# A one-core decoder layer: output-projection factors of w_out built in two passes, the mixture stored by token halves, pointwise input split between the projections

## The chip, the cores and the metric

The kernel runs on one core of a Trainium2 chip. Its time is the device time of one execution in microseconds; the median of the runs is compared. The profile is one execution of the program, recorded by the hardware profiler. Engines are named as there: PE is TensorE (matrix products), DVE is VectorE, ACT is ScalarE, POOL is GpSimd, and SP is SyncE, which here issues all the loads and stores.

## The reference

One layer over 1024 tokens with 1024 channels, all in float32. What is computed:

```
u   = rms_norm(x, ln_g)
z   = u @ w_in                                   # 1024 x 7168, split in seven blocks of 1024
c_val, c_glu, c_gate, hq, hf, hi, hg = split(z)
y_conv = silu(group_layer_norm(causal_conv31(c_val * sigmoid(c_glu)) + conv_b))
y_conv = (y_conv @ w_pw2 + b_pw2) * silu(c_gate) # the pointwise projection
y_hgrn = rms_norm(gated_recurrence(hq, hf, hi)) * silu(hg)   # 8 heads of 128
h   = x + concat(y_conv, y_hgrn) @ w_out         # w_out is 2048 x 1024
pe  = p @ w_pp
h   = h + sigmoid(rms_norm(h, pe_norm_g) @ w_pg) * pe
out = rms_norm(h, final_g)
```

## The kernel before, in words

Every float32 product is made of three: each operand is split into a high part, rounded on ACT, and the rest, subtracted on DVE (`split`, lines 117 to 119), and PE adds high by high, high by low and low by high. On chip, channels stand in partitions and tokens in the free dimension, in tiles of 128 by 512.

The program has these stages. Up to about 738 us: the input norm, then for each of eight heads the blocks of z (`ztile`, 48 matmuls each: 8 channel blocks, 3 products, 2 token halves), the convolution and the recurrence. Their tiles are in the pool wk. The last blocks of z are the eight gates c_gate (`conv_gate`, lines 492 to 496, numbers 16 to 23), stored to DRAM as sg_d. Then follow, in the program's text, `combos` (line 553), the projection of the heads' mixture yh_d (lines 662 to 671), the pointwise projection (683 to 705), the projection of the other mixture mc_d (753 and 754), and the last gate with the final norm.

The projection with w_out is done by a Winograd form of Strassen's scheme: for two blocks of 128 tokens `project` makes seven products of 12 matmuls in place of eight. Its factors from the mixture (w11, s1, s2, s4, s3, w12, w22) are sums of blocks, made by `tokens` (line 606); its factors from w_out (a, t1, t2, d, t3, c, t4) are made by `combos` for the lower and the upper thousand rows of w_out in turn: of each four 128x512 blocks a, b, c, d of a k, t1 = a - b, t2 = -(t1 + d), t3 = d - b, t4 = t1 + d - c. Each factor is split into high and low: 56 tiles of 128x512 in the pool cb, 112 KB of each partition. They are placed on the right end of SBUF, above the memory of the heads that have ended. Rows of w_out are loaded 128x1024 at a time: those of the first `combos` into the ring "raw" of the pool wp, three buffers that also take the gates' weights from `prep` (line 121); those of the second into the ring "raw" of rg, two buffers.

`project` reads the mixture from DRAM as two tiles (channels 0 to 511 and 512 to 1023 of 256 tokens) through the ring "raw" of rg; its products are added to two tiles of x, hx, one buffer each, and stored as h_d. rg lies on the left, in the memory of wp and of u, which the last gate reads. After the four projections, the 16 tiles of y_conv (ycr) are loaded through the ring "s" of rg and split into ych and ycl, 32 tiles of yp that the pointwise projection reads. It runs over m, the block of 128 output channels; its result, times the gate, is stored as 128 rows of mc_d (line 705), and then all of h_d is loaded back.

The order on each engine is the tile framework's: it takes the program's order, changed by priorities (`high_priority`; AHEAD and SOON are such distances), and inserts the waits. A tile waits for the last use of what lay in its memory before, tile by tile. Each engine and SP run their instructions in that order, so a waiting load holds those behind it.

Of the kernel before, what the change touches and what calls it, by code (L numbers as in the profile page):

```python
# [16 lines left out]
P = 128  # L17
T = 1024
D = 1024
G = 8  # L20
# [10 lines left out]
AHEAD, SOON = 500, 1000  # L31
# [6 lines left out]
def trunk_kernel(ctx: ExitStack, tc: tile.TileContext, x, p, ln_g, w_in, conv_w, conv_b,  # L38
# [16 lines left out]
    def halves(t):  # L55
        return t[:, :H], t[:, H:]
# [8 lines left out]
    mc_d = dpl.tile([D, T], F32, name="mc_d")  # L65
# [485 lines left out]
    cb = ctx.enter_context(tc.tile_pool(name="cb", bufs=1, side="right", reuse_waits="tile"))  # L551

    def combos(row0, pool, bufs):

        hi = {n: [] for n in XN}
        lo = {n: [] for n in XN}

        def part(n, k, src, sign=1.0):
            hi[n].append(cb.tile([P, H], F32R, tag=f"{n}h{k}", name=f"{n}h{row0}_{k}"))
            lo[n].append(cb.tile([P, H], F32R, tag=f"{n}l{k}", name=f"{n}l{row0}_{k}"))  # L560
            h = hi[n][k]
            nc.scalar.activation(h, src, AF.Copy, scale=sign)
            nc.vector.scalar_tensor_tensor(lo[n][k], src, sign, h.bitcast(F32),
                                           op0=ALU.mult, op1=ALU.subtract)

        for k in range(KH):
            rows = []
            for i in range(2):
                r = pool.tile([P, D], F32, tag="raw", bufs=bufs, name=f"wo{row0}_{k}_{i}")
                o = row0 + (i * KH + k) * P  # L570
                nc.sync.dma_start(r, w_out[o:o + P, :])
                rows += halves(r)
            a, b, c, d = rows
            for n, t in (("a", a), ("c", c), ("d", d)):
                part(n, k, t)
            nc.vector.tensor_tensor(a, a, b, op=ALU.subtract)
            part("t1", k, a)
            nc.vector.tensor_tensor(a, a, d, op=ALU.add)
            part("t2", k, a, -1.0)
            nc.vector.tensor_tensor(b, d, b, op=ALU.subtract)  # L580
            part("t3", k, b)
            nc.vector.tensor_tensor(c, a, c, op=ALU.subtract)
            part("t4", k, c)
        return hi, lo

    for m in range(G // 2):
        conv_gate(m)
    xh, xl = combos(D, wp, 3)
# [4 lines left out]
    rg = ctx.enter_context(tc.tile_pool(name="rg", bufs=4, reuse_waits="tile"))  # L593
# [12 lines left out]
    def tokens(src, tb):  # L606

        r0, r1 = (raw(src[i * H:(i + 1) * H, tb * P:(tb + 2) * P]
                      .rearrange("(k p) t -> p k t", p=P), f"mx{src.name}{tb}_{i}")
                  for i in range(2))  # L610
        w11, w21, w12, w22 = r0[:, :, :P], r0[:, :, P:], r1[:, :, :P], r1[:, :, P:]

        def add(n, x, y):
            o = rg.tile([P, KH, P], F32, tag="s", name=f"s{src.name}{tb}_{n}")
# [7 lines left out]
        return [factor(f"f{src.name}{tb}_{n}", t)  # L622
                for n, t in enumerate((w11, s1, s2, s4, s3, w12, w22))]

    def project(src, tb, hA, hB):

        f1, f5, f6, f3, f7, f2, f4 = tokens(src, tb)
        za, zd, zb = (bank("z", f"o{n}{src.name}{tb}") for n in "adb")

# [32 lines left out]
    with tc.tile_pool(name="hx", bufs=1, reuse_waits="tile") as hx:  # L662
        for tb in range(0, G, 2):
# [8 lines left out]
        ych = [[None] * G, [None] * G]  # L672
        ycl = [[None] * G, [None] * G]
        for hf in range(2):
            for k in range(G):
                ych[hf][k] = yp.tile([P, H], F32R, tag="y", name=f"ych{hf}_{k}")
                ycl[hf][k] = yp.tile([P, H], F32R, tag="y", name=f"ycl{hf}_{k}")
                t = rg.tile([P, H], F32, tag="s", name=f"ycr{hf}_{k}")
                nc.sync.dma_start(t, yc_d[k][:, hf * H:(hf + 1) * H])
                split(ych[hf][k], ycl[hf][k], t)  # L680


    with tc.tile_pool(name="sp", bufs=2, reuse_waits="tile") as sgp:
        for m in range(G):
            if m == 1:
                xh, xl = combos(0, rg, 2)
# [18 lines left out]
            nc.sync.dma_start(mc_d[m * P:(m + 1) * P, :], sg)  # L705
# [9 lines left out]
    def norm_T(hf, tags):  # L715
# [3 lines left out]
        for k in range(G):  # L719
# [5 lines left out]
            hh[k] = cb.tile([P, H], F32R, tag=f"{n}h{kk}", name=f"hh{hf}_{k}")  # L725
            hl[k] = cb.tile([P, H], F32R, tag=f"{n}l{kk}", name=f"hl{hf}_{k}")
# [29 lines left out]
    hhA, hlA = norm_T(0, ("a", "t1"))  # L756
    gate_weights(1, lambda q, k, name: cb.tile([P, H], F32R, tag=f"{('t2', 'd')[k // KH]}{q}{k % KH}",
                                               name=name))
    hhB, hlB = norm_T(1, ("c", "t4"))
# [67 lines left out]
```

## Time and profile before

| what | us |
|---|---|
| median of 3 runs (lowest, highest) | 1214.06 (1213.29, 1214.9) |
| the profiled execution's own time | 1217.44 |
| its span, first to last instruction | 1215.6 |
| PE busy, share of the span | 1124.5, 92% |
| DVE busy | 817.2, 67% |
| ACT busy | 461.5, 38% |
| mean granted clock of PE | 0.965 |

Busy times are sums over an engine's instructions. The granted clock is a share of 2.4 GHz; the two levels that the rows show are the full one and half of it. In the page's slices a digit is the busy share of one fortieth of the span, 30.4 us, in tenths. In lists of waits a row gives the waiting engine, what it made, what it waited for, then the sum in us, how many times, and the longest.

### The profile page before, as it was taken

The numbers are of one execution on the slowest core, as the hardware profiler recorded it, in microseconds if no ns is written. First come the engines' busy times: TensorE is split into PE (matmuls) and PEld (weight loads), VectorE is DVE, ScalarE is ACT, GpSimd is POOL, SyncE is SP. The second block draws the span as 40 slices with busy tenths as digits, with TensorE's granted clock in tenths as the row PEclk, the third lists the DMA queues.
The fourth block names the chain that finished last, engine by engine and source line by source line (L and its number), as shares of the span: only waits on it lengthen the run. The fifth ranks groups of instructions, "written<-read, shape, count | busy, mean of one in ns | idle before, by whom it ended". The sixth has DMA issues, their size and how long they took to land.

```text
span 1215.6 us, 17917 instructions
## 1 busy us (share of the span) xinstructions
PE 1124.5 (92%) x7312; PEld 935.9 (77%) x7312; DVE 817.2 (67%) x1305; ACT 461.5 (38%) x867; POOL 73.2 (6%) x107
## 2 busy tenths in 40 slices
PE   7999999999999999999999992688996994999997
PEld 5889888789788898888988882576675883887886
DVE  4669399995799965999849946405476721566644
ACT  4732254532443433435335325302143310226533
POOL 3100001010010100100100100000000000000100
PEclk9999999999999999999999996798997997999999
DMA  7511111211211121121121213324367545223221
GB/s 253 203 52 35 53 53 54 69 53 36 70 52 54 36 63 59 36 69 37 53 61 45 88 53 104 104 80 130 137 233 233 191 138 207 70 88 121 70 104 70
DMA packets 94547, 112.98 MB, mean 93 GB/s; under 512 B 3930, under 2 KB 74586, under 8 KB 94466
## 3 DMA queue, kind: packets, MB, share of 16 engines
q1 hardware_dynamic: 94466, 111.85, 28.2%
q8 instruction: 57, 0.93, 0.3%
q14 instruction: 24, 0.20, 0.0%
HBM read 82.48 MB, written 29.36 MB: 92 GB/s over the span
## 4 chain that ended last, share of the span: by engine, by line
PE 77%; DVE 10%; DMA 10%; ACT 2%; issue 1%; SPq 1%; POOL 0%; POOLq 0%; DVEq 0%; ACTq 0%
PE z L246 13%; PE z L247 13%; PE z L248 13%; DVE y L457 4%; PE v L270 3%; PE v L269 3%; PE v L268 3%; PE pw L700 3%; PE pw L701 2%; PE pw L702 2%; PE pg L780 2%; PE pg L779 2%; PE pg L778 2%; DMA mxyh_d<-yh_d 1%; PE sc L300 1%; DMA mxmc_d<-mc_d 1%
## 5 line engine op out<-in xcount | busy, mean ns | idle before, releaser
L457 DVE SCALAR_TENSOR_TENSOR y<-vpad,par,y 128x1024 f32<-128x1024 f32 x232 | 288.7, 1278 | 1.1
L778 PE MATMUL pg<-gh,hh 128*128 128x512 f32 (+1 forms) x136 | 52.3, 385 | 1.6 <-ACT hh L727 1.6
L779 PE MATMUL pg<-gl,hh 128*128 128x512 f32 (+1 forms) x136 | 52.4, 385 | 0.0
L780 PE MATMUL pg<-gh,hl 128*128 128x512 f32 (+1 forms) x136 | 52.1, 383 | 0.0
L524 DVE TENSOR_TENSOR vpad<-z,gl 128x512 f32<-128x512 f32 x16 | 11.0, 690 | 42.7 <-PE z L248 42.7
L246 PE MATMUL z<-uh,wz20h 128*128 128x512 f32 x16 | 7.6, 474 | 32.1 <-ACT wz20h L118 32.1
L700 PE MATMUL pw<-ych,wpw_0h 128*128 128x512 f32 x64 | 26.0, 407 | 11.6 <-ACT wpw_0h L118 11.6
L268 PE MATMUL v<-wv_0h,uh 128*128 128x256 f32 x128 | 36.7, 287 | 0.0
L270 PE MATMUL v<-wv_0h,ul 128*128 128x256 f32 x128 | 36.5, 285 | 0.0
L269 PE MATMUL v<-wv_0l,uh 128*128 128x256 f32 x128 | 36.5, 285 | 0.0
L270 PE MATMUL v<-wv_1h,ul 128*128 128x256 f32 x128 | 36.2, 283 | 0.0
L268 PE MATMUL v<-wv_1h,uh 128*128 128x256 f32 x128 | 36.2, 283 | 0.0
L269 PE MATMUL v<-wv_1l,uh 128*128 128x256 f32 x128 | 36.2, 283 | 0.0
L271 ACT ACTIVATE vt<-v 128x256 f32<-128x256 f32 x32 | 12.2, 382 | 59.0 <-PE v L270 59.0
L784 DVE TENSOR_TENSOR gt<-gt,pet 128x512 f32<-128x512 f32 (+1 forms) x17 | 11.2, 661 | 33.9 <-ACT gt L783 33.9
L480 DVE TENSOR_SCALAR y<-yt,mv,ry 128x128 f32<-128x128 f32 x64 | 23.5, 403 | 13.1 <-POOL ry L114 13.1
L113 POOL TENSOR_SCALAR ro<-sso 128x8 f32<-128x8 f32 x8 | 8.4, 1055 | 389.0 <-ACT on L134 389.0
L704 DVE SCALAR_TENSOR_TENSOR sgr<-pw,par,sgr 128x512 f32<-128x512 f32 x16 | 12.0, 747 | 29.3 <-PE pw L702 29.3
L778 PEld LDWEIGHTS pg<-gh,hh 128*128 128x128 f32 x136 | 25.8, 189 | 6.9 <-ACT hh L727 1.8
L442 ACT ACTIVATE on<-o,ro 128x128 f32<-128x128 f32 x64 | 18.6, 387 | 29.6 <-POOL ro L114 29.6
L779 PEld LDWEIGHTS pg<-gl,hh 128*128 128x128 f32 x136 | 25.8, 189 | 4.9
L780 PEld LDWEIGHTS pg<-gh,hl 128*128 128x128 f32 x136 | 25.7, 189 | 5.0
(698 smaller groups left out, 3551.5 us busy)
## 6 DMA issues: line engine op xcount, KB each, us to landing
wz<-in_w_in_dram SPq DMA_DIRECT2D x48, 512.0 KB
wo<-in_w_out_dram SPq DMA_DIRECT2D x16, 512.0 KB
xt<-in_x_dram SPq DMA_DIRECT2D x8, 512.0 KB
pe_d<-pes SPq DMA_DIRECT2D x8, 512.0 KB
wv<-in_w_in_dram SPq DMA_DIRECT2D x8, 512.0 KB
yc_d<-yc SPq DMA_DIRECT2D x8, 512.0 KB
yh_d<-sgT SPq DMA_DIRECT2D x8, 512.0 KB
sg_d<-sgc SPq DMA_DIRECT2D x8, 512.0 KB
```

Of the source, the lines that this page charges most:

```text
L246: mm(z, lhsT=wh[:, k, :], rhs=mh[hf][k], start=k == 0, stop=False)
L247: mm(z, lhsT=wh[:, k, :], rhs=ml[hf][k], start=False, stop=False)
L248: mm(z, lhsT=wl[:, k, :], rhs=mh[hf][k], start=False, stop=k == G - 1)
L268: mm(z, lhsT=uh[hf][k][:, c], rhs=wh, start=k == 0, stop=False)
L269: mm(z, lhsT=uh[hf][k][:, c], rhs=wl, start=False, stop=False)
L270: mm(z, lhsT=ul[hf][k][:, c], rhs=wh, start=False, stop=k == G - 1)
L457: nc.vector.scalar_tensor_tensor(y[j % 2], vp[:, j:j + T], pcol(g, j), y[j % 2], op0=ALU.mult, op1=ALU.add)
L700: mm(z, lhsT=wh, rhs=ych[hf][k], start=k == 0, stop=False)
L701: mm(z, lhsT=wh, rhs=ycl[hf][k], start=False, stop=False)
L778: mm(z, lhsT=hh[k][:, c], rhs=gh[j][k][:, o:o + w], start=k == 0, stop=False)
L779: mm(z, lhsT=hh[k][:, c], rhs=gl_[j][k][:, o:o + w], start=False, stop=False)
L780: mm(z, lhsT=hl[k][:, c], rhs=gh[j][k][:, o:o + w], start=False, stop=k == G - 1)
```

## The change

It has three parts.

First, the factors of the lower half of w_out are built in two passes. The pool cb keeps a, t1, t2, d and t3 only (80 KB), and rg, with the rings for rows and for factors, moves to the right, next to it, in the heads' memory. The first pass (`combos(D, False, whole_rows(D))`) loads its rows there, in a ring of two, and makes these five. The factors c and t4 get a pool cc on the left, where wp was, and are made by a second pass (`combos(D, True, quarter_rows(D))`) in front of the projections; it loads the same rows again as 16 tiles of 128x512 into buffers of yp. Second, the mixture of the pointwise stage is stored as two tensors, one of each half of the tokens, as soon as that half of a channel block is done. Third, the 16 loads and splits of y_conv are done four after each projection. Of AHEAD, the distance by which the pointwise weights are taken earlier, 500 becomes 1500.

```diff
-AHEAD, SOON = 500, 1000
+AHEAD, SOON = 1500, 1000
-    mc_d = dpl.tile([D, T], F32, name="mc_d")
+    mc_d = [dpl.tile([D, H], F32, name=f"mc_d{hf}") for hf in range(2)]
     cb = ctx.enter_context(tc.tile_pool(name="cb", bufs=1, side="right", reuse_waits="tile"))
-    def combos(row0, pool, bufs):
+    rg = ctx.enter_context(tc.tile_pool(name="rg", bufs=4, side="right", reuse_waits="tile"))
+    cc = None
+    def combos(row0, late, rows):
         def part(n, k, src, sign=1.0):
-            hi[n].append(cb.tile([P, H], F32R, tag=f"{n}h{k}", name=f"{n}h{row0}_{k}"))
-            lo[n].append(cb.tile([P, H], F32R, tag=f"{n}l{k}", name=f"{n}l{row0}_{k}"))
+            if late is not None and late != (n in ("c", "t4")):
+                return
+            pool = cc if n in ("c", "t4") else cb
+            hi[n].append(pool.tile([P, H], F32R, tag=f"{n}h{k}", name=f"{n}h{row0}_{k}"))
+            lo[n].append(pool.tile([P, H], F32R, tag=f"{n}l{k}", name=f"{n}l{row0}_{k}"))
...
-            for n, t in (("a", a), ("c", c), ("d", d)):
-                part(n, k, t)
+            a, b, c, d = rows(k)
+            part("a", k, a)
+            part("d", k, d)
             nc.vector.tensor_tensor(a, a, b, op=ALU.subtract)
             part("t1", k, a)
             nc.vector.tensor_tensor(a, a, d, op=ALU.add)
             part("t2", k, a, -1.0)
-            nc.vector.tensor_tensor(b, d, b, op=ALU.subtract)
-            part("t3", k, b)
-            nc.vector.tensor_tensor(c, a, c, op=ALU.subtract)
-            part("t4", k, c)
+            if late is not True:
+                nc.vector.tensor_tensor(b, d, b, op=ALU.subtract)
+                part("t3", k, b)
+            if late is not False:
+                part("c", k, c)
+                nc.vector.tensor_tensor(c, a, c, op=ALU.subtract)
+                part("t4", k, c)
+    def whole_rows(row0):
+        def rows(k):
+            res = []
+            for i in range(2):
+                r = rg.tile([P, D], F32, tag="raw", bufs=2, name=f"wo{row0}_{k}_{i}")
+                o = row0 + (i * KH + k) * P
+                nc.sync.dma_start(r, w_out[o:o + P, :])
+                res += halves(r)
+            return res
+        return rows
+    def quarter_rows(row0):
+        def rows(k):
+            res = []
+            for i in range(4):
+                r = yp.tile([P, H], F32, tag="y", name=f"wq{row0}_{k}_{i}")
+                o = row0 + (i // 2 * KH + k) * P
+                nc.sync.dma_start(r, w_out[o:o + P, i % 2 * H:(i % 2 + 1) * H])
+                res.append(r)
+            return res
+        return rows
     for m in range(G // 2):
         conv_gate(m)
-    xh, xl = combos(D, wp, 3)
+    xh, xl = combos(D, False, whole_rows(D))
     for m in range(G // 2, G):
         conv_gate(m)
     zx.close()
-    rg = ctx.enter_context(tc.tile_pool(name="rg", bufs=4, reuse_waits="tile"))
+    cc = ctx.enter_context(tc.tile_pool(name="cc", bufs=1, reuse_waits="tile"))
...
     with tc.tile_pool(name="hx", bufs=1, reuse_waits="tile") as hx:
+        lh, ll = combos(D, True, quarter_rows(D))
+        for n in ("c", "t4"):
+            xh[n], xl[n] = lh[n], ll[n]
...
-            project(yh_d, tb, *hAB)
+            project(yh_d, tb * P, f"yh{tb}", *hAB)
             for i in range(2):
                 nc.sync.dma_start(h_d[tb + i], hAB[i])
-        for hf in range(2):
-            for k in range(G):
+            for i in range(4):
+                hf, k = tb // 4, tb % 4 * 2 + i
                 ych[hf][k] = yp.tile([P, H], F32R, tag="y", name=f"ych{hf}_{k}")
                 ycl[hf][k] = yp.tile([P, H], F32R, tag="y", name=f"ycl{hf}_{k}")
-                t = rg.tile([P, H], F32, tag="s", name=f"ycr{hf}_{k}")
+                if tb < G - 2:
+                    t = yp.tile([P, H], F32, tag="y", name=f"ycr{hf}_{k}")
+                else:
+                    t = hx.tile([P, H], F32, tag="yr", name=f"ycr{hf}_{k}")
                 nc.sync.dma_start(t, yc_d[k][:, hf * H:(hf + 1) * H])
                 split(ych[hf][k], ycl[hf][k], t)
...
-                xh, xl = combos(0, rg, 2)
+                xh, xl = combos(0, None, whole_rows(0))
...
-            nc.sync.dma_start(mc_d[m * P:(m + 1) * P, :], sg)
+                nc.sync.dma_start(mc_d[hf][m * P:(m + 1) * P, :], s)
...
-        project(mc_d, tb, hs[tb], hs[tb + 1])
+        project(mc_d[tb // 4], tb % 4 * P, f"mc{tb}", hs[tb], hs[tb + 1])
```

`tokens` and `project` take the first token's column and a name in place of the block's number, and the second `norm_T` puts its tiles in cc.

The order of SP around the end of the heads, before: wo1024 are rows of w_out, wz20 to wz23 the weights of gates 20 to 23, yh_d the store of the last head's output, sg_d4 the store of gate 20.

```order
L450 DMA yh_d_89<-sgT7_6021 128x1024
L571 DMA wo1024_1_1_6947<-in_w_out_dram 128x1024
L571 DMA wo1024_2_0_6981<-in_w_out_dram 128x1024
L571 DMA wo1024_2_1_6983<-in_w_out_dram 128x1024
L571 DMA wo1024_3_0_7017<-in_w_out_dram 128x1024
L571 DMA wo1024_3_1_7019<-in_w_out_dram 128x1024
L124 DMA wz20_7054<-in_w_in_dram 128x8x128
L124 DMA wz21_7114<-in_w_in_dram 128x8x128
L124 DMA wz22_7174<-in_w_in_dram 128x8x128
L124 DMA wz23_7234<-in_w_in_dram 128x8x128
```

And after the change, on SP, from two loads of gate weights to the second pair of rows:

```order
L124 DMA wz22_7142<-in_w_in_dram 128x8x128
L496 DMA sg_d1_74<-sgc1_6733 128x1024
L124 DMA wz23_7202<-in_w_in_dram 128x8x128
L490 DMA yc_d7_88<-yc7_6384 128x1024
L496 DMA sg_d2_75<-sgc2_6793 128x1024
L496 DMA sg_d3_76<-sgc3_6853 128x1024
L450 DMA yh_d_89<-sgT7_6022 128x1024
L596 DMA wo1024_0_0_6913<-in_w_out_dram 128x1024
L596 DMA wo1024_0_1_6915<-in_w_out_dram 128x1024
L496 DMA sg_d4_77<-sgc4_7021 128x1024
L596 DMA wo1024_1_0_6940<-in_w_out_dram 128x1024
L596 DMA wo1024_1_1_6942<-in_w_out_dram 128x1024
```

The gate weights now all stand ahead of the last head's store, and the rows of w_out behind it.

The order of DVE in the first projection, before, up to the sums for the second one (fyh_d_890 are the mixture's factors, hx0 and hx1 the tiles of x, oayh_d and odyh_d products in PSUM):

```order
L119 TENSOR_TENSOR fyh_d_890_5l_7341<-mxyh_d_890_1_7310,fyh_d_890_5h_7340 128x512
L643 TENSOR_TENSOR hx0_7304<-hx0_7304,oayh_d_890_7348 128x512
L119 TENSOR_TENSOR fyh_d_890_6l_7345<-mxyh_d_890_1_7310,fyh_d_890_6h_7344 128x512
L643 TENSOR_TENSOR hx0_7304<-hx0_7304,odyh_d_890_7349 128x512
L119 TENSOR_TENSOR fyh_d_892_0l_7461<-mxyh_d_892_0_7448,fyh_d_892_0h_7460 128x512
L615 TENSOR_TENSOR syh_d_892_1_7452<-mxyh_d_892_0_7448,mxyh_d_892_1_7450 128x512
```

And after the change, on DVE, the end of the first projection's part (wq1024 are the quarter rows, cl and t4l the low parts of c and t4):

```order
L569 SCALAR_TENSOR_TENSOR cl1024_3_7340<-wq1024_3_2_7333,ch1024_3_7339 128x512
L569 SCALAR_TENSOR_TENSOR t4l1024_2_7326<-wq1024_2_2_7314,t4h1024_2_7325 128x512
L578 TENSOR_TENSOR wq1024_3_0_7329<-wq1024_3_0_7329,wq1024_3_3_7335 128x512
L669 TENSOR_TENSOR hx0_7348<-hx0_7348,obyh0_7394 128x512
L585 TENSOR_TENSOR wq1024_3_2_7333<-wq1024_3_0_7329,wq1024_3_2_7333 128x512
L119 TENSOR_TENSOR ycl0_0_7489<-ycr0_0_7490,ych0_0_7488 128x512
L641 TENSOR_TENSOR syh2_1_7520<-mxyh2_0_7516,mxyh2_1_7518 128x512
L569 SCALAR_TENSOR_TENSOR t4l1024_3_7345<-wq1024_3_2_7333,t4h1024_3_7344 128x512
```

The second pass stands between the first projection's factors and the second's; from the first factor's low part to the last row here are 39 operations.

The order of SP at the end of the pointwise stage, before (mxmc_d_900_1 is the load of channels 512 to 1023 for the first projection, h0 to h7 the loads of h_d):

```order
L705 DMA mc_d_90<-sgr6_8522 128x1024
L705 DMA mc_d_90<-sgr7_8589 128x1024
L711 DMA h0_8649<-h_d0_91 128x1024
L711 DMA h1_8650<-h_d1_92 128x1024
L711 DMA h2_8651<-h_d2_93 128x1024
L711 DMA h3_8652<-h_d3_94 128x1024
L711 DMA h4_8653<-h_d4_95 128x1024
L711 DMA h5_8654<-h_d5_96 128x1024
L711 DMA h6_8655<-h_d6_97 128x1024
L711 DMA h7_8656<-h_d7_98 128x1024
L597 DMA mxmc_d_900_1_8667<-mc_d_90 128x4x256
```

And after the change:

```order
L737 DMA mc_d0_90<-sgr6_8572 128x512
L737 DMA mc_d1_91<-sgr6_8572 128x512
L737 DMA mc_d0_90<-sgr7_8640 128x512
L623 DMA mxmc0_1_8719<-mc_d0_90 128x4x256
L737 DMA mc_d1_91<-sgr7_8640 128x512
L743 DMA h0_8701<-h_d0_92 128x1024
L743 DMA h1_8702<-h_d1_93 128x1024
```

The load of the mixture now stands ahead of the loads of h and of the last store of the second half.

## Rows read from the trace of the kernel before

**Rows 1.** The page's slices: 40 equal parts of the span, busy tenths, granted clock.

```profile
PE   7999999999999999999999992688996994999997
PEclk9999999999999999999999996798997997999999
```

**Rows 2.** Waits of PE from 700 us on: who waited for whom, sum, times, longest.

```profile
PE z L246 <- ACT wz20h L118: 32.1, 1, 32.1
PE odmc_d L633 <- ACT fmc_d_1h L118: 15.3, 1, 15.3
PE pw L700 <- ACT wpw_0h L118: 11.6, 1, 11.6
PE oayh_d L633 <- ACT fyh_d_0h L118: 8.3, 1, 8.3
PE oayh_d L633 <- DVE hx L643: 2.0, 3, 1.3
PE pg L778 <- ACT hh L727: 1.6, 1, 1.6
```

**Rows 3.** Timeline: start, duration, engine, line, operation, tiles, idle time before and its end.

```profile
736.97 1.03 PE L446 MATMUL ot<-ident,on 128*128 128x128 f32 x8
...
739.04 0.32 SPq L450 DMA_DIRECT2D yh_d<-sgT  x1
...
770.12 0.79 PE L246 MATMUL z<-uh,wz20h 128*128 128x512 f32 x1 [32.12 <-ACT wz20h L118]
...
816.35 0.60 ACT L495 ACTIVATE sgc<-z 128x512 f32<-128x512 f32 x1 [4.79 <-PE z L248]
...
824.61 0.80 PE L633 MATMUL oayh_d<-ah,fyh_d_0h 128*128 128x512 f32 x1 [8.30 <-ACT fyh_d_0h L118]
```

**Rows 4.** Timeline of PE, the last three matmuls of the pointwise stage.

```profile
1012.04 0.39 PE L700 MATMUL pw<-ych,wpw_1h 128*128 128x512 f32 x1
1012.27 0.39 PE L701 MATMUL pw<-ycl,wpw_1h 128*128 128x512 f32 x1
1012.49 0.39 PE L702 MATMUL pw<-ych,wpw_1l 128*128 128x512 f32 x1
```

**Rows 5.** Chain of waits from 700 us on: start, length, what; a DMA's from issue.

```profile
741.41 0.60 DVE al L563
...
746.26 3.63 DMA wo<-in_w_out_dram
...
817.86 5.99 DMA mxyh_d<-yh_d
...
845.64 4.03 DMA h_d<-hx
...
865.88 5.62 DMA h_d<-hx
...
1019.13 10.35 DMA mxmc_d<-mc_d
...
1031.00 0.79 PE odmc_d L633
1031.79 0.43 PE odmc_d L635
```

**Rows 6.** Busy time by stretch: projections, their end, pointwise, the last stage's start.

```profile
core 0: us, PE busy (x) PEld busy (x) DVE busy (x) ACT busy (x) POOL busy (x), PEclk, DMA share, GB/s
824.60:911.00 86.40, 82.90 (x336) 64.02 (x336) 54.82 (x86) 25.78 (x43) 0.00 (x0) 0.97 0.47 159
900.00:920.00 20.00, 11.08 (x47) 8.38 (x46) 17.70 (x28) 11.24 (x20) 0.00 (x0) 0.88 0.80 276
922.60:1012.70 90.10, 90.06 (x384) 74.28 (x385) 42.52 (x65) 21.88 (x37) 0.00 (x0) 0.97 0.49 161
1100.00:1120.00 20.00, 18.33 (x88) 14.89 (x87) 14.46 (x23) 12.54 (x25) 0.74 (x2) 0.91 0.37 118
```

**Rows 7.** Timeline of DVE and SP at the end of the pointwise stage.

```profile
1012.92 0.75 DVE L704 SCALAR_TENSOR_TENSOR sgr<-pw,par,sgr 128x512 f32<-128x512 f32 x1 [4.69 <-PE pw L702]
...
1014.06 5.03 SPq L711 DMA_DIRECT2D h<-h_d  x8
...
1029.51 0.69 DVE L615 TENSOR_TENSOR smc_d<-mxmc_d,mxmc_d 128x512 f32<-128x512 f32 x1 [10.03 <-DMA mxmc_d<-mc_d]
```

More of the change, by code (lines that the diff above doesn't have):

```diff
@@ L566, in combos @@
         for k in range(KH):
[L567 to L573, printed above, removed]
-            for n, t in (("a", a), ("c", c), ("d", d)):
-                part(n, k, t)
+            a, b, c, d = rows(k)
+            part("a", k, a)
+            part("d", k, d)
             nc.vector.tensor_tensor(a, a, b, op=ALU.subtract)
@@ L604, in factor, with tokens @@
         return hi, lo
-    def tokens(src, tb):
-        r0, r1 = (raw(src[i * H:(i + 1) * H, tb * P:(tb + 2) * P]
-                      .rearrange("(k p) t -> p k t", p=P), f"mx{src.name}{tb}_{i}")
+    def tokens(src, col, key):
+        r0, r1 = (raw(src[i * H:(i + 1) * H, col:col + 2 * P]
+                      .rearrange("(k p) t -> p k t", p=P), f"mx{key}_{i}")
                   for i in range(2))
@@ L613, in add @@
         def add(n, x, y):
-            o = rg.tile([P, KH, P], F32, tag="s", name=f"s{src.name}{tb}_{n}")
+            o = rg.tile([P, KH, P], F32, tag="s", name=f"s{key}_{n}")
             nc.vector.tensor_tensor(o, x, y, op=ALU.add)
@@ L621, in tokens, with project @@
         s3 = add(3, w11, w21)
-        return [factor(f"f{src.name}{tb}_{n}", t)
+        return [factor(f"f{key}_{n}", t)
                 for n, t in enumerate((w11, s1, s2, s4, s3, w12, w22))]
-    def project(src, tb, hA, hB):
-        f1, f5, f6, f3, f7, f2, f4 = tokens(src, tb)
-        za, zd, zb = (bank("z", f"o{n}{src.name}{tb}") for n in "adb")
+    def project(src, col, key, hA, hB):
+        f1, f5, f6, f3, f7, f2, f4 = tokens(src, col, key)
+        za, zd, zb = (bank("z", f"o{n}{key}") for n in "adb")
         def mul(z, f, n, first, last):
@@ L662, in trunk_kernel @@
     with tc.tile_pool(name="hx", bufs=1, reuse_waits="tile") as hx:
+        lh, ll = combos(D, True, quarter_rows(D))
+        for n in ("c", "t4"):
+            xh[n], xl[n] = lh[n], ll[n]
+        ych = [[None] * G, [None] * G]
+        ycl = [[None] * G, [None] * G]
         for tb in range(0, G, 2):
@@ L713, in trunk_kernel, with norm_T @@
     rs = [None] * G
-    def norm_T(hf, tags):
+    def norm_T(hf, pool, tags):
         hh = [None] * G
@@ L724, in norm_T @@
             n, kk = tags[k // KH], k % KH
-            hh[k] = cb.tile([P, H], F32R, tag=f"{n}h{kk}", name=f"hh{hf}_{k}")
-            hl[k] = cb.tile([P, H], F32R, tag=f"{n}l{kk}", name=f"hl{hf}_{k}")
+            hh[k] = pool.tile([P, H], F32R, tag=f"{n}h{kk}", name=f"hh{hf}_{k}")
+            hl[k] = pool.tile([P, H], F32R, tag=f"{n}l{kk}", name=f"hl{hf}_{k}")
             nc.scalar.activation(hh[k], pt, AF.Copy, scale=pcol(k, R_PE))
@@ L753, in trunk_kernel @@
     for tb in range(0, G, 2):
-        project(mc_d, tb, hs[tb], hs[tb + 1])
+        project(mc_d[tb // 4], tb % 4 * P, f"mc{tb}", hs[tb], hs[tb + 1])
     gate_weights(0, lambda q, k, name: hp.tile([P, H], F32R, name=name))
-    hhA, hlA = norm_T(0, ("a", "t1"))
+    hhA, hlA = norm_T(0, cb, ("a", "t1"))
     gate_weights(1, lambda q, k, name: cb.tile([P, H], F32R, tag=f"{('t2', 'd')[k // KH]}{q}{k % KH}",
                                                name=name))
-    hhB, hlB = norm_T(1, ("c", "t4"))
+    hhB, hlB = norm_T(1, cc, ("c", "t4"))
     fg = hp.tile([P, D], F32, name="fg")
```

2 lines of the change are left out of this document (removed).

## The prediction

> **What bounds the kernel now.** Three views, in this order. First the page's slices [rows 1]: PE is busy for nine tenths or more in every slice from the second to the twenty-fourth, so the part up to about 738 us is TensorE's own work; after it the row has holes (2, 6, 6, 4), and the granted clock falls in or next to them. Then PE's waits from 700 us on [rows 2]: four long ones, each in one piece: 32.1 us for the first gate weights after the heads, 8.3 us for the first factor of the heads' mixture, 11.6 us for the first pointwise weights, 15.3 us for the second factor of the other mixture. That is 67.3 us of idle TensorE, each wait behind a load. Then the lines around them [rows 3, 7] say what the load itself stood behind. TensorE is done with the heads at about 738 (736.97 + 1.03) and starts gate 20 at 770.12; the loads of the gates' weights follow eight loads of w_out in the same ring of row buffers. The last gate's rows are done about 816.3, and the first projection starts at 824.61. Pointwise ends at 1012.7, and the second factor's input lands only at 1029.5, because its load is queued behind eight loads of h that were issued from 1014.06 to 1019.1.
>
> **Prices.** A matmul of 512 columns follows the one before it after 0.227 us at the high level of the clock (mean of 1012.04, 1012.27 and 1012.49) [rows 4] and after 0.43 us at the low one (the piece at 1031.79) [rows 5]. One start at the low level costs 2.7 us: gates 20 to 23 are 192 matmuls, 43.5 us at 0.227, and took 46.2 (770.12 to 816.35) [rows 3]. Pointwise is 384 matmuls, 87.1 us at 0.227, and took 90.1 [rows 6]: 3.0 us. A load of 512 KB that nothing is ahead of takes 3.6 us, a store of h 4.0, DVE starts a 128x512 operation every 0.60 us [rows 5], and an activation of that size lasts 0.60 on ACT [rows 3]. A load behind eight others took 10.35 us; those nine, 4.7 MB, were through 15.5 us after the first issue (1014.06 to 1029.5), 0.30 MB per us [rows 5, 7].
>
> **Part 1, factors of w_out in two passes.** In the order before, eight loads of w_out stand ahead of the gate weights 20 to 23; in the new one the gate weights stand before the last head's store and w_out has a ring of its own. So gate 20 starts when the heads end, at 738, and the 32.1 us go, with the 2.7 us of the low clock: minus 34.8. Gates end at 738 + 43.5 = 781.5.
>
> Next late is the first pass, which DVE used to do while TensorE was idle. Its first load stands behind the store of the last head (739.04), which now follows one more split on DVE, of 128x1024 (1.2 us, twice 0.60): issue 740.6, landed 744.2. The rows' ring holds one pair, so each of the four pairs is load, then work. The first pair meets the split of gate 23's weights in ACT's and DVE's order, and that needs the buffer that gate 20 frees at 738 + 10.9 = 748.9; four operations stand behind it, and the pair ends near 754.4. Each later pair is 3.6 us for the first load, 1.2 for the second one behind it and eight DVE operations with one ACT step ahead (4.8 + 0.6), of which about 0.6 overlaps: 9.6 us. 754.4 + 3 x 9.6 = 783.2; the mixture's load follows in the same ring, 3.6 to 4: landed 787.3, and TensorE starts 0.7 later at 788.0. It idles 6.5 us where it idled 8.3: minus 1.8. I take the low clock after it as before, no change there.
>
> The second pass loads 16 quarter rows (4.2 MB) after 785, with 0.8 MB ahead of them: at 0.30 MB per us the last lands near 804, 17 us after the factor. DVE is later than that: from the first factor to the last factor of w_out stand 39 DVE operations in its order, 39 x 0.60 + 0.7 = 24 us, and the last products wait for them. The first projection is 84 matmuls, 19.0 us at 0.227; before, the four took 86.4 us with the low clock and 3.5 us of waits [rows 6], so about 20 each beside that. Now the first takes 24 + 4 = 28 with the low clock's lag in DVE's operations on PSUM. No row shows such a chain; its ends are 0 (products of the next projection fill in, as the order starts to do) and 16 more (all sixteen loads waited for before any product: 16.5 us for 5.0 MB, less what is covered). I take the middle, plus 7 or so.
>
> **Part 2, pointwise input split pair by pair.** 16 loads of 256 KB and 16 splits move from after the fourth projection to between them; the pointwise weights are prepared ahead (AHEAD 1500). The 11.6 us go and the 3.0 us of the low clock with them: minus 14.6. The cover is the projections: DVE was busy 54.8 of 86.4 us there [rows 6]; with 16 x 0.60 for the splits, 20 operations of the second pass at 0.60 and 3 us for the first weights it is about 80 of 90. DMA moved 159 GB/s in it; with 4.2 MB of quarter rows, most of 4.2 MB of input rows and 1 to 2 MB of weights it is about 250, where 276 stood beside a busy share of 0.80 [rows 6]. So each chain "h stored, x loaded" (4.0 + 3.6) gets longer. I give projections 2 to 4 20.4, 19.5 and 20, and 2 for that: the stage is 28 + 60 + 2 = 90 against 86.4, plus 3.6. Its ends are minus 3 (no idle) and plus 25 (each chain twice as long, 3 x 8).
>
> **Part 3, mixture by token halves.** The load of the second factor's rows needs only the first half of each channel block, which ends 24 matmuls (5.4 us) before pointwise does, and in SP's order it stands ahead of the h loads. Counted from the end E of pointwise: half done E - 5.4, DVE 0.75 [rows 7], store issued E - 4.4, done E - 1.0 (256 KB, between nothing and the 4.0 of 512 KB; I take 3.4, nearest to the row), load landed E + 2.6, sum and split E + 4. TensorE has 12 matmuls (2.7 us) to do first. Before, it went on 18.3 us after E (1012.7 to 1031.0) [rows 4, 5]; now 4: minus 14.3. The idle left is about 1.3 us. Three waits of up to 1.3 inside the projections left the clock at 0.97 with its low start counted, one of 1.6 stands in a stretch at 0.91 [rows 2, 6]; nearest to the first, I take the start at the low level as gone: minus 2.9, and 0 as the other end. The eight more stores wait on SP for DVE; behind them stand rows of the gate buffer, which have two blocks (21 us) of slack, so nothing there. The ends: 0 saved if the load still waits for the second half, 16 at best.
>
> The h loads are late next: h0 lands at E + 5.5 where DVE reaches it at E + 8, so a microsecond is lost there, inside the 4.
>
> **Sum.** -34.8 - 1.8 + 3.6 - 14.6 - 14.3 - 2.9 = -64.8. The profiled execution took 1217.4 us (span 1215.6): 1152.6. It lies 3.4 above the median of the runs, 1214.06, from which the sum is 1149.3. I say 1150.
>
> **Rivals.**
> A, the projections become bound by DVE and DMA. For it: both busy shares above 0.8 by the counts above, and h and x have one buffer each, so a late load stops the put that TensorE waits for. Against it: the order has the loads a projection ahead. Price: 15 to 25 us, 1165 to 1175.
> B, quarter rows are paid one after the other, so that all of the first projection's last two products wait for all sixteen loads: 16 us, 1166. Against it: eight loads left SP in 5.0 us and the ninth, issued behind them, landed 10.35 us after its issue, so transfers overlap [rows 5, 7]. The Trainium skill, page DMA: Bandwidth & Descriptors, speaks for it: its section Anatomy of one DMA gives every transfer (there issued by GpSimd) a fixed part of about 2.0 us beside its bytes over 436 GB/s, and its section Rules for kernel authors asks for 1 MiB or more. An estimate from that page is 2.6 us for 256 KB, 41.6 us for sixteen in turn, after which the first projection would end 17 us later than I have it; the trace agrees with the size of the fixed part (3.6 us for 512 KB), not with paying it in turn.
> C, the change does not do what it says at one place: the second factor still waits for the whole mixture, or the gate weights for their ring. The order speaks against both. Price 15 (or 35): 1165, or 1185.
> D, slower than before. One mechanism: SP issues in order, and the projections' loads of x now stand between loads that wait for buffers which the same projection frees. If each projection must end before the next can load, its length is 19 + 5.6 (store) + 3.6 (x) + 6.0 (mixture, queued) + 2.7 (sum and split) = 37 instead of 20: 4 x 17 = 68, and the second pass's 16 behind the same queue: 1150 + 68 - 7 + 16 = 1227. It decides from about 18 us lost per projection. Against it: DVE's order reads each load several operations after what frees its issue.
>
> **Chances.** The forecast 0.66 (own range 1137 to 1163, from a stage of 82 to 100 us and a first wait of 2 to 9); A 0.18; B 0.05; C 0.06; D 0.03, and 0.02 for less than 1137. The range must hold eight in ten: 1136 to 1172 takes the forecast and most of A and B. About 0.2% (2.4 us) is what a measurement can tell from no change. Faster: all but D, 0.96; same 0.01; slower 0.03.
>
> **What would show it.** Gate 20's first matmul within 2 us of the last head's; PE's wait for the first factor between 3 and 9 us; waits of the first projection for t4 and c factors, 4 to 9 us together; no wait over 3 us at the first pointwise matmul; the second factor 3 to 7 us after pointwise's end; the low clock once in place of four times. Wrong would be: a wait of 10 us or more on x or the mixture in projections 2 to 4 (A, D), or a second factor that follows the h loads (C).

## The result, and the profile after

The changed kernel takes 1151.68 us, median of 3 runs (1150.76 to 1151.84), against 1214.06: a ratio of 0.9484, 95% interval 0.9462 to 0.9505. The forecast was 1150 us, with a range of 1136 to 1172. Beside the experiments it was timed again: 0.9492 (0.9476 to 0.9508). The profiled execution took 1151.84 us with a span of 1150.1; before they were 1217.44 and 1215.6.

From the page of the changed kernel, PE's busy tenths and granted clock in 40 slices:

```profile
PE   6999999999999999999999999998999999999997
PEclk9999999999999999999999999999999999999999
```

The four slices in which PE had long been idle in [rows 1] (busy for 2, 6, 6 and 4 tenths) are gone, and no slice's clock is under 0.9 any more. Shorter windows show that the low level did not go altogether. From the heads' end to the last microseconds it stands three times, for 3.4 us each (the columns are those of [rows 6]; the clock, behind the bracket of POOL, is 0.50 or 0.51):

```profile
785.10:788.50 3.40, 3.21 (x8) 2.50 (x9) 1.44 (x3) 0.18 (x2) 0.00 (x0) 0.50 0.89 275
812.40:815.80 3.40, 3.40 (x9) 2.56 (x9) 3.40 (x7) 1.54 (x3) 0.00 (x0) 0.51 0.82 266
1048.00:1051.40 3.40, 3.40 (x16) 2.95 (x14) 3.02 (x5) 2.12 (x4) 0.00 (x0) 0.50 0.00 0
```

PE's waits from 700 us on, as [rows 2] were of before:

```profile
PE oayh L659 <- ACT fyh_0h L118: 3.8, 1, 3.8
PE oayh L659 <- ACT t4h L568: 2.8, 3, 1.3
PE pg L810 <- ACT hh L759: 2.2, 1, 2.2
PE obyh L659 <- ACT fyh_5h L118: 1.2, 2, 0.7
PE oayh L661 <- DVE t4l L569: 0.6, 1, 0.6
PE obmc L659 <- ACT fmc_5h L118: 0.5, 1, 0.5
```

The waits of 32.1 for gate 20, of 11.6 for the pointwise weights and of 15.3 for odmc have no successor. What is new is small: 3.4 us for t4 factors, the price of the second pass.

The timeline of the changed kernel from the heads' end to the end of the first projection, as [rows 3] were:

```profile
736.85 1.03 PE L446 MATMUL ot<-ident,on 128*128 128x128 f32 x8
737.64 0.47 PE L246 MATMUL z<-uh,wz20h 128*128 128x512 f32 x1
...
740.49 1.19 SPq L596 DMA_DIRECT2D wo<-in_w_out_dram  x2
...
761.96 10.94 SPq L596 DMA_DIRECT2D wo<-in_w_out_dram  x4
...
781.19 1.72 SPq L623 DMA_DIRECT2D mxyh<-yh_d  x2
...
785.28 0.80 PE L659 MATMUL oayh<-ah,fyh_0h 128*128 128x512 f32 x1 [3.83 <-ACT fyh_0h L118]
785.47 13.27 SPq L607 DMA_DIRECT2D wq<-in_w_out_dram  x16
...
811.72 0.39 PE L663 MATMUL oayh<-t4h,fyh_6l 128*128 128x512 f32 x1
```

Gate 20 begins 0.8 us after the start of the heads' last transposes. The rows of w_out are loaded beside the gates, the mixture is asked for at 781.19, and the first projection runs from 785.28 to 811.95 (the last row and 0.23 of a product): 26.7 us. In it DVE is the engine that hardly rests. Windows of the changed kernel: from DVE's first sum to the last t4 product, and pointwise, its own instructions alone, so that the second row has only the columns of PE, PEld and DVE ahead of the clock (12 products of the last projection stand between those of pointwise):

```profile
core 0: us, PE busy (x) PEld busy (x) DVE busy (x) ACT busy (x) POOL busy (x), PEclk, DMA share, GB/s
787.70:812.00 24.30, 20.78 (x83) 15.01 (x82) 23.95 (x40) 10.52 (x17) 0.00 (x0) 0.98 0.88 322
...
872.20:964.60 92.40, 89.67 (x384) 72.03 (x384) 11.14 (x15) 1.00 0.55 175
```

And the end of pointwise (E = 964.46 + 0.23 = 964.7), which answers to [rows 4, 5, 7]:

```profile
959.29 0.75 DVE L736 SCALAR_TENSOR_TENSOR sgr<-pw,par,sgr 128x512 f32<-128x512 f32 x1 [4.85 <-PE pw L734]
960.07 0.32 SPq L737 DMA_DIRECT2D mc_d<-sgr  x1
962.15 0.37 SPq L623 DMA_DIRECT2D mxmc<-mc_d  x1
964.46 0.40 PE L734 MATMUL pw<-ych,wpw_1l 128*128 128x512 f32 x1
965.67 0.32 SPq L737 DMA_DIRECT2D mc_d<-sgr  x1
966.04 4.45 SPq L743 DMA_DIRECT2D h<-h_d  x8
967.42 0.39 PE L659 MATMUL odmc<-t1h,fmc_1h 128*128 128x512 f32 x1
```

The first half is stored at 960.07, its load leaves SP at 962.15, ahead of the second half's store and of the h loads, and the second factor's first product starts 2.7 us after E without a wait.

The span by stage, from the start times of the first or last product of each in the two profiled executions:

| from | to | before, us | after, us | difference | forecast |
|---|---|---|---|---|---|
| start | last transposes of the heads (736.97; 736.85) | 737.0 | 736.9 | -0.1 | 0 |
| there | last gate product (815.92; 781.06) | 78.9 | 44.2 | -34.7 | -34.8 |
| there | first product of a projection (824.61; 785.28) | 8.7 | 4.2 | -4.5 | -1.8 |
| there | last pointwise product (1012.49; 964.46) | 187.9 | 179.2 | -8.7 | -11.0 |
| there | first product of the second factor (1031.00; 967.42) | 18.5 | 3.0 | -15.5 | -14.3 |
| there | first product of the last stage (1111.84; 1046.89) | 80.8 | 79.5 | -1.4 | -2.9 |
| there | end of the span (1215.6; 1150.1) | 103.8 | 103.2 | -0.6 | 0 |
| sum | | | | -65.5 | -64.8 |

### The profile page after: what moved, and what is told of

It reads as the page before. It is cut to its first block, busy times and chain, and to the rows that moved or that the text cites. A ratio compares the mean times of both kernels' runs of the same rounds, so it can differ in the third digit from the quotient of the medians.

```text
span 1150.1 us, 17964 instructions
## 1 busy us (share of the span) xinstructions
PE 1119.0 (97%) x7312; PEld 930.5 (81%) x7312; DVE 821.6 (71%) x1313; ACT 460.4 (40%) x867; POOL 73.1 (6%) x107
## 4 chain that ended last, share of the span: by engine, by line
PE 79%; DVE 9%; DMA 8%; ACT 2%; issue 1%; SPq 0%; POOL 0%; POOLq 0%; ACTq 0%; DVEq 0%
PE z L246 13%; PE z L247 13%; PE z L248 13%; DVE y L457 4%; PE v L269 3%; PE v L268 3%; PE v L270 3%; PE pg L810 3%; PE pw L732 3%; PE pw L734 3%; PE pw L733 3%; PE pg L812 3%; PE pg L811 3%; DMA mxyh<-yh_d 1%; PE sc L300 1%; DMA wo<-in_w_out_dram 1%
## 5 line engine op out<-in xcount | busy, mean ns | idle before, releaser
L271 ACT ACTIVATE vt<-v 128x256 f32<-128x256 f32 x32 | 12.2, 381 | 59.0 <-PE v L270 59.0
L488 ACT ACTIVATE yc<-yn,par 128x512 f32<-128x512 f32 x16 | 12.5, 778 | 37.6 <-PE yn L487 37.6
L134 ACT ACTIVATE on<-o 128x128 f32<-128x128 f32 x64 | 16.8, 278 | 23.3 <-PE up L414 18.9
```

## The experiments

Each run is beside runs of the kernel before on the same chip; its ratio to that is what is compared, since that kernel's median was 1212.0 to 1213.2 there. A per mille of the ratio is 1.2 us; the intervals are about 1.5 per mille to each side, so a difference of two ratios is known to about 2.

**One part undone at a time.** whole_mixture takes part 3 back:

```diff
-                nc.sync.dma_start(mc_d[hf][m * P:(m + 1) * P, :], s)
+            nc.sync.dma_start(mc_d[m * P:(m + 1) * P, :], sg)
```

> The changed kernel with the mixture stored whole again, one store of 128x1024 per channel block (part 3 undone; parts 1 and 2 kept). Theory: part 3 is worth what the prediction gave it, so TensorE waits 14 to 15 us for the second factor (it waits 0 now) and starts the last projections at the low clock, 2.9 us: 1151.7 + 17.5 = 1169 us. Rival: those products only come earlier and wait later for h or for the third factor, so part 3 is worth a few us: 1155 to 1159.

Measured: 1165.55 us, 0.9617 (0.9602 to 0.9631), 12.5 per mille or 15.2 us above the changed kernel's 0.9492. PE waits 15.8 us for the second factor. The wait is the theory's (14 to 15 us) and the rival falls; the whole is 15.2 us and not the 17.5 that the theory made of it with the low clock. From the timeline of whole_mixture (E = 963.3), with the second factor's first product last:

```profile
964.24 0.32 SPq L737 DMA_DIRECT2D mc_d<-sgr  x1
964.61 5.07 SPq L743 DMA_DIRECT2D h<-h_d  x8
969.73 0.45 SPq L623 DMA_DIRECT2D mxmc<-mc_d  x1
...
980.42 0.69 DVE L641 TENSOR_TENSOR smc<-mxmc,mxmc 128x512 f32<-128x512 f32 x1 [10.07 <-DMA mxmc<-mc_d]
...
981.91 0.79 PE L659 MATMUL odmc<-t1h,fmc_1h 128*128 128x512 f32 x1 [15.77 <-ACT fmc_1h L118]
```

The mixture's load leaves SP behind the eight h loads and then takes 10.7 us beside them (969.73 to DVE's start at 980.42). whole_mixture_h_late changes only that order:

```diff
+        if tb is not None:
+            nc.sync.dma_start(hA, h_d[tb])
+            nc.sync.dma_start(hB, h_d[tb + 1])
...
-    for tb in range(G):
-        nc.sync.dma_start(hs[tb], h_d[tb])
```

> As whole_mixture, but the eight h loads stand behind the first mixture loads in SP's order, two per projection. It tells the two halves of part 3 apart: that the load no longer needs the last half block, and that it no longer stands behind eight h loads. Theory: both count. Last DVE operation at E + 1, store landed at E + 5, load landed 4 to 5 us later at E + 9.5, sum and split at E + 11; TensorE has 2.7 us to do, so it waits 8 us: 1151.7 + 8 + 0 to 2.9 = 1160 to 1163 us. Rival 1, the order behind the h loads was all: 1152 to 1154. Rival 2, the dependence on the whole block was all: 1168 to 1170.

Measured: 1156.89 us, 0.9549 (0.9535 to 0.9563). Its timeline (E = 966.3):

```profile
967.29 0.32 SPq L740 DMA_DIRECT2D mc_d<-sgr  x1
969.96 0.37 SPq L623 DMA_DIRECT2D mxmc<-mc_d  x1
...
973.37 0.69 DVE L641 TENSOR_TENSOR smc<-mxmc,mxmc 128x512 f32<-128x512 f32 x1 [6.11 <-DMA mxmc<-mc_d]
...
974.86 0.79 PE L662 MATMUL odmc<-t1h,fmc_1h 128*128 128x512 f32 x1 [5.66 <-ACT fmc_1h L118]
```

Both halves of part 3 count: of its 12.5 per mille, 6.8 are the place behind the h loads (0.9617 to 0.9549), 5.7 the dependence on the last half block. They were taken apart in this order only: half stores behind the h loads were not run. The wait was 5.7 us where I expected 8: the store let the load go after 2.7 us, and the load landed 3.4 us later, not 4 to 5.

late_split takes part 2 back:

```diff
-            for i in range(4):
-                hf, k = tb // 4, tb % 4 * 2 + i
+        for hf in range(2):
+            for k in range(G):
...
-                if tb < G - 2:
-                    t = yp.tile([P, H], F32, tag="y", name=f"ycr{hf}_{k}")
-                else:
-                    t = hx.tile([P, H], F32, tag="yr", name=f"ycr{hf}_{k}")
+                t = rg.tile([P, H], F32, tag="s", name=f"ycr{hf}_{k}")
```

> The changed kernel with the sixteen loads and splits of the pointwise input back behind the fourth projection, with a row buffer in the ring of the sums as before (part 2 undone but for the 1500 of AHEAD; in the changed kernel's own order 500 and 1500 give the same instructions on every engine). Theory: the wait of 11.6 us and the 3.0 us of low clock come back, and the projections get 1 to 3 us shorter without those loads: 1151.7 + 12.5 = 1164 us. Rival 1: the weights being ready (AHEAD) was what counted: 1153 to 1156. Rival 2: the splits slow the projections by as much as they save: 1152 to 1156.

Measured: 1162.77 us, 0.9593 (0.9579 to 0.9608): 10.1 per mille, 12.2 us. The wait is back with AHEAD at 1500, so the split's place is what counts. PE's longest wait in late_split:

```profile
PE pw L729 <- ACT wpw_0h L118: 11.6, 1, 11.6
```

one_pass takes part 1 back:

```diff
-    xh, xl = combos(D, False, whole_rows(D))
+    xh, xl = combos(D, wp, 3)
...
-        lh, ll = combos(D, True, quarter_rows(D))
```

> The kernel before with parts 2 and 3 alone: all seven factors of w_out made in one pass, from rows in the gate weights' ring, behind which four gates wait (part 1 undone). Theory: the terms of part 1 are separate from the others: 32.1 of wait, 2.7 of low clock and 1.8 at the first factor come back, 3.6 of the longer first projection go: 1151.7 + 33 = 1185 us. Rival: the second pass costs the projections more than the first one's 26 us, through DMA and DVE shared with the splits, so without it they are 5 to 8 us shorter: 1177 to 1180.

Measured: 1185.31 us, 0.9781 (0.9764 to 0.9797): 28.9 per mille, 35.0 us. PE's two longest waits in one_pass:

```profile
PE z L246 <- ACT wz20h L118: 32.0, 1, 32.0
PE oayh L633 <- ACT fyh_0h L118: 9.0, 1, 9.0
```

The three parts alone add up to 12.5 + 10.1 + 28.9 = 51.5 per mille; together they gave 50.8 (1 - 0.9492). Within the intervals they do not share a gain. one_pass takes back the whole of part 1; whether putting the gate weights ahead of the rows of w_out, without a second pass, would have been enough was not run.

> The changed kernel itself, beside the other kernels of this group, so that they are compared on one chip: 0.9484 of the kernel before, as measured first (0.9462 to 0.9505).

Measured: 1152.35 us, 0.9492 (0.9476 to 0.9508), as told above.

**What limits the first projection.** c_rows_only makes the second pass cheaper:

```diff
+            if late:
+                c = rows(k)
+                part("c", k, c)
+                s = hx.tile([P, H], F32, tag="yr", name=f"t2s{row0}_{k}")
+                nc.vector.tensor_tensor(s, xh["t2"][k].bitcast(F32), xl["t2"][k].bitcast(F32), op=ALU.add)
+                nc.vector.scalar_tensor_tensor(c, s, -1.0, c, op0=ALU.mult, op1=ALU.subtract)
+                part("t4", k, c)
+                continue
...
+            r = yp.tile([P, H], F32, tag="y", name=f"wq{row0}_{k}")
+            o = row0 + (KH + k) * P
+            nc.sync.dma_start(r, w_out[o:o + P, :H])
```

> The changed kernel with a cheaper second pass: t4 = -(t2h + t2l) - c from the factor of the first pass that is in memory already, so that only the quarter of w_out that holds c is loaded (4 loads in place of 16), and DVE does 4 operations per row block in place of 5. Theory, the first projection is bound by DVE: 4 x 0.60 = 2.4 us less between the first factor and the last t4 factor, of 3.4 us of waits, so 2.4 us faster than the changed kernel, 0.2%. Rival 1, the sixteen loads bind it (3.1 MB less to move): all of the first projection's lost 7 us goes, 5 to 7 us faster. Rival 2, the wait for x and the mixture of the second projection takes its place: 0 to 1 us.

Measured: 1149.60 us, 0.9478 (0.9465 to 0.9491), 1.4 per mille below the changed kernel, with intervals that overlap. PE's waits in c_rows_only:

```profile
PE oayh L664 <- ACT fyh_0h L118: 3.8, 1, 3.8
PE oayh L664 <- DVE hx L674: 3.0, 1, 3.0
PE obyh L664 <- ACT fyh_5h L118: 2.1, 2, 1.1
PE pg L815 <- ACT hh L764: 2.0, 1, 2.0
PE oayh L668 <- DVE fyh_0l L119: 1.2, 1, 1.2
```

The waits for t4 (3.4 us) are gone, but those for x (3.0, where changed_again has 0.7), for the mixture's factors of the c products (2.1, there 1.2) and for the next mixture's first factor (1.2, there none) grew by 4.4 in all; from the first product of a projection to the first of pointwise it is 87.7 us for 88.0. Twelve loads fewer (3.1 MB) brought nothing that shows, so rival 1 falls; rival 2 took most of what DVE gave. The first projection by itself did get shorter, 25.6 us for 27.2, although the low level lasted 6 us in it in place of 3.4: DVE's operations were its bound, and what they gave back was lost behind it.

**Why pointwise won nothing from the clock.** It ran at a clock of 1.00 after and at 0.97 before, and yet its 384 products took 89.67 us against 90.06 [rows 6]. The products start 0.2333 us apart in the changed kernel's pointwise and 0.2267 in that of before; in the projections it is mostly the other way round. Part 1 moved the pool of the stationary factors, so I took the place in memory for the cause. pw_weights_low puts seven eighths of the pointwise weights on the side where the moving operands are (the gate rows change place for it, and the order of the products within a channel block changes):

```diff
+                    hi = sgp.tile([P, KH, P], F32R, tag="hi", bufs=3, name=f"wpw{m}_{i}h")
+                    lo = sgp.tile([P, KH, P], F32R, tag="lo", name=f"wpw{m}_{i}l")
+                    split(hi, lo, t)
...
```

> The changed kernel with the stationary factors of seven of the eight pointwise channel blocks in the lower half of SBUF's addresses, where the moving operands lie (the gate rows take their ring; both output halves of a block go through one weight factor before the other, but for the last block). Theory: a 128x512 product starts 0.2267 us after the one before where both operands lie in one half of the addresses, and 0.2333 where they do not, so 336 x 0.0066 = 2.2 us faster than the changed kernel, 0.19%. Rival: the cadence of pointwise comes from the DMA and DVE traffic of that stage, not from the place: no change, within 0.1%.

Measured: 1147.24 us, 0.9459 (0.9446 to 0.9472); the interval lies below the changed kernel's, on the same chip. Its 384 products take 87.67 us, 2.0 less:

```profile
872.00:963.40 91.40, 87.67 (x384) 72.10 (x384) 11.20 (x15) 1.00 0.55 180
```

In this one trace the 48 products of the first channel block, whose weights stayed, are 0.2334 us apart, and the 336 of the others 0.2267. Part of the rest of the 3.3 per mille goes with the clock: the profile of changed_again has the low level for 3.4 us at the start of the last stage, where this run's has 1.00, and its last stage takes 103.3 us for 101.9 here. What is left I can't place. The place does something, then, but not as I thought:

> A series of products alone: 36 groups of 96 products of 128x512, in the same pattern of three as in the kernel, with the moving and the stationary operand each at 6, 54, 110, 118, 166 and 214 KB of SBUF's 224 KB per partition; all else of the computation is left out. Theory: 0.2267 us from start to start in the 18 groups with both operands below 112 KB or both above, 0.2333 in the other 18. Rival 1: it goes with the distance of the two, or with the place of one of them alone. Rival 2: the place does not matter, and all 36 groups have one cadence, since nothing else runs here.

Measured: all 36 groups took 0.2266 or 0.2267 us per product. DVE copies the result of each group of 96; the copies for moving 6 KB with stationary 110 and 118 KB:

```profile
94.54 0.69 DVE L57 COPY o<-m_s 128x512 f32<-128x512 f32 x1 [21.07 <-PE m_s L56]
116.30 0.69 DVE L57 COPY o<-m_s 128x512 f32<-128x512 f32 x1 [21.07 <-PE m_s L56]
```

(116.30 - 94.54) / 96 = 0.2267, with the operands in different halves. The two halves of the memory make no difference. What both theories had overlooked: in places every operand began on a multiple of 512 bytes from the same base, while in the changed kernel the left pools begin on a multiple of 64 bytes and the right ones 32 past one.

> A series of products alone, as places, but with the moving and the stationary operand shifted by 0, 16, 32, 48, 64 and 96 bytes each from addresses that are multiples of 64 bytes (moving near 2 KB, stationary near 162 KB); all else of the computation is left out. In places all operands began on multiples of 64 bytes and all 36 groups took 0.2267; in the changed kernel the pools on the left begin on multiples of 64 bytes and those on the right 32 bytes past one. Theory: what counts is whether the two operands begin at the same place within 64 bytes: 0.2267 us from start to start in the groups where they do (0 with 0 and 64, 32 with 32 and 96, 16 with 16, 48 with 48), 0.2333 where they lie 32 bytes apart (0 or 64 with 32 or 96). Rival 1: an operand off a multiple of 64 bytes costs by itself, whatever the other one is. Rival 2: no offset matters alone, all 36 groups have 0.2267, and it takes the traffic of the other engines as well.

Measured, from the times of DVE's copies at the end of each group of 96. In the timeline of offsets, the copies of the groups with moving 0 and stationary 0, 16 and 32 follow that of a warming group:

```profile
30.55 0.69 DVE L57 COPY o<-warm 128x512 f32<-128x512 f32 x1 [30.55 <-PE warm L56]
52.31 0.69 DVE L57 COPY o<-m_s 128x512 f32<-128x512 f32 x1 [21.07 <-PE m_s L56]
74.08 0.69 DVE L57 COPY o<-m_s 128x512 f32<-128x512 f32 x1 [21.08 <-PE m_s L56]
96.47 0.69 DVE L57 COPY o<-m_s 128x512 f32<-128x512 f32 x1 [21.70 <-PE m_s L56]
```

(52.31 - 30.55) / 96 = 0.2267 for 0 and 0, (96.47 - 74.08) / 96 = 0.2332 for 0 and 32. Of the offsets that are multiples of 32, the four equal pairs took 0.2267 to 0.2270 and eleven of the twelve others 0.2332 to 0.2343 (96 with 32: 0.2291). So equal starts are fast and 32 bytes apart slow, as the theory said; but 64 bytes apart is slow too (0.2332), which it had wrong. With a shift of 16 or 48 bytes the theory fails: 16 with 16 took 0.2300 and 48 with 48 took 0.2332, although they begin at the same place, and the groups range from 0.2267 to 0.2365. One order is there: with the moving operand shifted by 0, 32 or 64, a stationary one 16 bytes away is as fast as an equal one (0.2267 to 0.2269 in four groups). Rival 2 falls, since no other engine's traffic is needed. Rival 1 falls for 32 bytes past a multiple of 64 (32 with 32 is fast); for 16 and 48 it is open.

changed_aligned shifts all left pools by 32 bytes, so that both sides begin at the same place within 512:

```diff
+    even = ctx.enter_context(tc.tile_pool(name="even", bufs=1))
+    nc.gpsimd.memset(even.tile([P, G], F32, name="even"), 0.0)
```

> The changed kernel with one tile of 32 bytes per partition ahead of the large pools, so that those on the left too begin 32 bytes past a multiple of 64, as those on the right do; no other edit, the same instructions but for one memset. Theory of the alignment: 384 pointwise products, 192 of the factors c and t4 and about half of the last stage's 384 go from 0.2333 to 0.2267: 768 x 0.0066 = 5.1 us, so 0.9492 of the kernel before becomes 0.945. Rival, it is the half of the memory and not the alignment: no change, 0.949.

Measured: 1147.33 us, 0.9474 (0.9461 to 0.9487). The products of pointwise in changed_aligned:

```profile
873.00:962.80 89.80, 87.13 (x384) 71.97 (x384) 11.13 (x15) 1.00 0.55 179
```

87.13 / 384 = 0.2269, against 89.67 / 384 = 0.2335: 2.5 us. Against the profile of changed_again, the two stages of projections are 0.3 us shorter each and the last stage 2.7; the span is 1145.1 against 1151.1. Of the 2.7 about half is the alignment's (192 x 0.0066 = 1.3 us). The other half goes with the clock, since changed_again has the low level at the start of its last stage and changed_aligned has 1.00 there:

```profile
1048.10:1051.50 3.40, 3.40 (x13) 2.49 (x13) 3.40 (x6) 2.12 (x4) 0.00 (x0) 0.50 0.00 0
```

The timed runs say less, 1.8 per mille by ratios whose intervals overlap; the sign is likely, the size open.

> The same tile with c_rows_only: theory, the two add up, 5.1 + 1.7 us below the changed kernel, 0.9435 of the kernel before. Rival: the faster products wait longer for DVE in the first projection, so that one of the two is lost: 0.945.

Measured: 1146.93 us, 0.9471 (0.9451 to 0.9490): nothing beyond changed_aligned. The theory's 0.9435 lies outside the interval; the rival is right that one of the two gains is lost, though its 0.945 is a little low too. Where it is lost was not looked into.

> The kernel before with the same tile. There the factors of the mixture lie on the left and all factors of w_out on the right, so that all 672 products of the projections are 32 bytes apart, and half of the last stage's 384, while pointwise is not. Theory of the alignment: 864 x 0.0066 = 5.7 us faster, 0.9953. It tells what part of the change's gain was a matter of addresses: by this the change won 480 x 0.0066 = 3.2 us in the projections and lost 384 x 0.0066 = 2.5 in pointwise. Rival: no change.

Measured: 1211.13 us over 12 runs, 0.9995 (0.9982 to 1.0009). The runs rule out the 5.7 us, although the products of its profiled execution are 0.2267 apart in the projections, where they were 0.2333. That execution (1207.09 us) was the fastest of the twelve. The mean granted clock of the runs is 0.965 for both kernels, so it isn't the clock that takes the gain; where the other executions spend it isn't to be seen without their traces. So the distance between products is shown to follow the addresses, but not that the kernel's time does.

## Why the prediction was right

**The gates** (-34.8): -34.7, with the wait and the low clock both gone. one_pass brought back 32.0 of wait.

**The first factor** (-1.8): -4.5 by the table; the wait is 3.8 where I had 6.5. The mechanism held, the start was mis-sized: I let the mixture's load wait for the last row buffer of the pair to be done with, at 783.2, but it left SP at 781.19, when DVE had done the sum a + d and one split of the pair was still to come (781.83).

**The projections** (90 us for 86.4): 89.8 (87.0 to pointwise's first product, and 12 products of the last projection that now stand inside pointwise, at 0.2333). The first took 26.7 for 28, and DVE was its bound, busy 23.95 of 24.3 us; the waits for t4 factors are 3.4 us, under the 4 to 9 forecast for t4 and c (4.6 with the two for the mixture's factor of the c products). c_rows_only shows DVE as that bound. Rival B, the quarter rows paid in turn, fails: sixteen loads left SP in 13.3 us, with DMA at 322 GB/s in that stretch, and the last t4 product started 26.3 us after the first of them. By the Trainium skill, page DMA: Bandwidth & Descriptors, section Anatomy of one DMA, the estimate for sixteen in turn was 41.6 us. The trace doesn't agree with paying the loads in turn. Rival A, DVE and DMA as the bound of the whole stage, holds for the first projection alone.

**Part 2** (-14.6): the wait of 11.6 is gone, and the clock of the stage is 1.00, but its 3.0 us did not show in the time. This is a term that was mis-sized: pointwise itself went only from 90.06 [rows 6] to 89.67, because its products start 0.2333 us apart in place of 0.2267 (384 x 0.0066 = 2.5 us), which I had taken to stay. In the profiles of pw_weights_low and changed_aligned 2.0 and 2.5 us of this came back.

**Part 3** (-14.3): -15.5. The store let its load go after 2.1 us (960.07 to 962.15), not 3.4, and there is no idle time left, where 1.3 us were forecast. Both reasons of the step, the half block and the order before the h loads, are shown by experiment, about half each. The low clock behind it (-2.9) gave -1.4 over that stage. This term was too large from the start, since in the kernel before the low level ended 3.7 us behind the wait, and half of that is 1.9:

```profile
1031.00:1034.70 3.70, 3.70 (x9) 2.88 (x10) 3.68 (x6) 1.86 (x3) 0.00 (x0) 0.51 0.12 33
```

The products of five of the seven factors also came to stand 0.2267 apart there, so more should have been won than 1.4; what took it was not looked into.

Three of the signs came out otherwise: the waits for t4 (3.4 us, not 4 to 9), the second factor 2.7 us behind E (not 3 to 7), and the low clock, which stands three times and not once. Two of the three pieces stand at the start and at the end of the first projection, and products start 0.43 us apart there: in the projections the low level lasts 6.6 us, where it lasted 5.2 before.

The sum was right within a microsecond for the two profiled executions (-65.5 for -64.8) because an early mixture and second factor (3.9 us more than forecast) met a slower pointwise and a smaller gain of clock (3.8 us less). That these cancel is luck. So is the choice of execution: by the medians the gain is 62.4 us, since the profiled execution of before lay 3.4 above its median. What was understood is that the three parts touch three different waits, whose gains add (51.5 per mille apart, 50.8 together); that is why the total held to within some microseconds.

## What to carry to other kernels

A wait in a ring shared by two streams goes when one of them gets a ring of its own, even if that costs a second pass over the data: here 4.2 MB loaded again and 8 DVE operations more (a - b and a + d, done twice) cost 3.4 us of waits and removed 32. When a result is stored for a reload, store it in the pieces in which it is read, and see what stands in front of the reload in the issuing queue: each gave about half of 15 us. After moving a pool, compare the distance between the starts of products before and after, not only the waits.

## What the runs showed of the hardware

The distance between the starts of 128x512 float32 products depends on where the two operands begin. With both on multiples of 32 bytes it is 0.2267 us if they begin at the same place within 512 bytes (36 groups of places, four of offsets, all of pointwise in changed_aligned), and 0.2333 if they lie 32, 64 or 96 bytes apart, 3% more (eleven of twelve groups of offsets). A stationary operand 16 bytes away from a moving one on a multiple of 32 was still fast (four groups); with the moving operand off by 16 or 48 even equal starts were slow (0.2300 and 0.2332), and why is open. A store of 256 KB to DRAM let the load of the same rows go 2.1 us after its own issue (the changed kernel), one of 512 KB 2.7 us (whole_mixture_h_late).
